# An interleaved decoder trunk on eight cores: first loads in one queue by need, a late query filler, and schedule priorities found by search

## The chip, the cores and the metric

The kernel runs on all eight cores of one Trainium2 chip. Each core computes its own piece of the sequence. The time is the device time of the slowest core, in microseconds (us). The program has a second, slower state, in which one die, or both, is granted a lower TensorE clock in the records (0.84 in one such execution, 3153 us).

## The reference, cut to what matters

```python
DEPTH = 4; D_MODEL = 1024; SEQ = 8192; BATCH = 2; N_META = 16
for i in range(DEPTH):                       # mixers: attention, convolution, pooling, attention
    a = rms_norm(h, norm_mix[i])
    m = (sliding_window_attention | short_conv_mixer | pooling_mixer)(a, ...)
    h = h + m
    h = h + swiglu(rms_norm(h, norm_ffn[i]), gate[i], up[i], down[i])   # the FFN
h = rms_norm(h, norm_final)
```

A norm needs the squares of all 1024 channels (ScalarE), their sum (a product with ones on TensorE), a reciprocal root (ScalarE) and eight multiplications (VectorE, tag `apply`) before the products behind it can start.

## The kernel before: the parts that matter

The activations stay on the core. The columns are split into three groups, and four layers by three groups make twelve steps. While one step's FFN runs, the next step's mixer can run beside it. The mixer of the first layer is attention: it needs three projections (products of the normed x with weights) called K, V and query, and K and V also of the halo, 192 columns of x from before the core's own piece. The kernel records every operation with a duration and a priority `v`, and when it is built, a list scheduler orders each engine's instructions. For each engine it looks for the earliest possible start, and among the operations that could start then it takes the lowest `v`:

```python
for t, o in cands:
    if t <= mt + 1e-6 and (bo is None or (o.pv, o.id) < (bo.pv, bo.id)):
        bo = o
...
if FILL and e == "pe" and t - free["pe"] > FILL_MIN:      # FILL_MIN = 1500 ns
    self.fill(free["pe"], t)        # 128x128 products of constants, result unread
```

The filler is meant to keep the clock of TensorE up: in the trace of the kernel before, the granted clock was at half from 19.7 to 33.3 us, around a bare wait of 9.3 us. Priorities follow a fixed rule: a mixer of step `s` is spread over `s` to `s + 0.8`, its FFN's norm has `s + 0.9`, the FFN is spread over `s + 1` to `s + 2`, and the final norm of a group has `s + 1.9`:

```python
def end_segment(g, v0, span):
    tot = sum(o.dur for o in g.seg if o.eng == "pe") or 1.0
    c = 0.0
    for o in g.seg:
        o.v = v0 + span * c / tot
        if o.eng == "pe":
            c += o.dur
```

Weights come through a ring buffer, issued by GpSimd in order of need. The activations and constants are issued by SyncE, and later x blocks wait for chosen operations:

```python
xa = load_x(0, 4, v=-9.0)                        # first x block, four pieces, SyncE
load(gam[:], gam_d, ["gam"], v=-8.95)            # eight more small constants like it
...
def LATER():                                     # next group's x, gated by the last statistics op
    w = [o for o in g.ops if o.tag == LTAG]
    w = [w[LIDX]]
    for t in (2, 3):
        load_x(t, 1, after=w, v=-8.0)
    load_tables(0, after=w, v=-7.9)
...
for t in (2, 3):                                 # query filler: the next group's query products
    norm_to(aM, "aM", 0, TILES[t][0], TILES[t][1], GROUPS[1][0], v=QB_NV)       # QB_NV = None
...
q_tile(u, 0, 1, c, TILES[t][0], TILES[t][1], v=QB_V)                            # QB_V = None
```

The softmax here doesn't subtract the row's maximum and nothing guards it: scores larger than these inputs give would overflow.

Of the kernel before, what the change touches and what calls it, by code (L numbers as in the profile page):

```python
# [11 lines left out]
KC = 8  # L12
# [15 lines left out]
SPAN = (0.8, 0.8, 0.8)  # L28
NV = (0.9, 0.9, 0.9)
ITERS = 1  # L30


def JIT(s, sp, nv):
    return sp, nv


VORDER = True
# [3 lines left out]
VOFF = 0.0  # L41
QB_AT = 0
LTAG = "stat"
LIDX = -1
UA = {0: (1,),1:(3,),2:(4,)}
QB_NV = None
QB_V = None
# [4 lines left out]
RING = 16400  # L52

# [91 lines left out]
class Op:  # L145
    __slots__ = ("eng", "dur", "ins", "raw", "war", "v", "vts", "nleft", "succ", "start", "fin", "vis", "idx", "ready",
                 "id", "dma", "clock", "pv", "extra", "nbytes", "unit", "tag")


class Unit:  # L150
    __slots__ = ("src", "n", "users", "left", "off", "order", "dop", "first", "v", "arr", "grp", "num")


class G:
    def __init__(self):
        self.ops = []
        self.keys = {}
        self.units = []
        self.v = 0.0
        self.seg = None  # L160
        self.unit_after = {}
# [7 lines left out]
    def op(self, eng, dur, ins, R=(), W=(), after=(), dma=None, unit=None, v=None, tag="", hold=(), war_after=(), gate=()):  # L169
# [7 lines left out]
        o.id = len(self.ops)  # L177
        raw = {}
# [65 lines left out]
        o.v = self.v if v is None else v  # L244
# [19 lines left out]
    def weights(self, src, n, grp=None):  # L264
        u = Unit()
        u.grp = grp if grp is not None else len(self.units)
        u.num = len(self.units)
        u.src = src
        u.n = n
        u.users = []  # L270
        u.first = None
        self.units.append(u)
        return u
# [6 lines left out]
def end_segment(g, v0, span):  # L280
    tot = sum(o.dur for o in g.seg if o.eng == "pe") or 1.0
    c = 0.0
    for o in g.seg:
        o.v = v0 + span * c / tot
        if o.eng == "pe":
            c += o.dur
    g.seg = None

# [36 lines left out]
class Scheduler:  # L325
# [30 lines left out]
    def run(self, ring_mode=True):  # L356
# [18 lines left out]
        for o in g.ops:  # L375
            for vt in o.vts:
                vt.left = len(vt.users)
                vt.slot = None
            if o.nleft == 0:
                ready[o.eng].append(o)  # L380
# [13 lines left out]
        def place():  # L394
# [3 lines left out]
            u = uorder[nu]  # L398
            off = ptr
# [15 lines left out]
            for q in g.unit_after.get(nu, ()):  # L415
                if q.start is None:
                    return None
                t = max(t, q.vis)
            return u, off, deps, max(t, pool_t)

        def issue(nxt):
            nonlocal nu, ptr, dma_t, pool_t
            u, off, deps, t = nxt
            dset = set(id(x) for x in deps)
            live[:] = [x for x in live if id(x[2]) not in dset]
            st = max(dma_t, t + 200.0)
            pool_t = max(t + 530.0, st - 12000.0)
# [4 lines left out]
            self.uload.append((u, deps, t, g.unit_after.get(nu, ())))  # L432
            live.append((off, u.n, u))
            ptr = off + u.n
            nu += 1

        gates = set(q.id for l in g.unit_after.values() for q in l)
        self.nfill = 0
        pool_t = 0.0
# [3 lines left out]
        while nsched < total:  # L443
# [39 lines left out]
            if nxt is not None and (best is None or nxt[3] <= best[0]):  # L483
                issue(nxt)
# [34 lines left out]
            if o.unit is not None:  # L519
                u = o.unit  # L520
                if u.first is None:
                    u.first = nsched
                    for q in u.users:
                        if q.start is None and q.pv > o.pv:
                            q.pv = o.pv
                u.left -= 1
            for vt in o.vts:
                vt.left -= 1
                if vt.left == 0:
                    self.pools[vt.pool].release(vt)  # L530
            for s, war in o.succ:
                r = o.vis + self.lat(o, s, war)
                if r > s.ready:
                    s.ready = r
                s.nleft -= 1
                if s.nleft == 0:
                    ready[s.eng].append(s)
            if ring_mode and nxt is None and ((o.unit is not None and o.unit.left == 0) or o.id in gates):
                nxt = place()
# [3 lines left out]
def late_starts(g, s, T):  # L543

    L = {}
    nxt = {}
    for e in ENGS:
        q = s.seq[e]
        for a, b in zip(q[:-1], q[1:]):
            nxt[a.id] = b  # L550
    xs = {}
    for o in g.ops:
        for q in o.extra:
            xs.setdefault(q.id, []).append(o)
    over = {}
    for i, (u, deps, st, after) in enumerate(s.uload):
        for u2 in deps:
            over.setdefault(id(u2), []).append(i)
    ldma = {}
    items = [(o.start, 1, o.id, o) for o in g.ops] + [(st, 0, i, u) for i, (u, d, st, af) in enumerate(s.uload)]  # L560
    items.sort(key=lambda x: (-x[0], x[1], -x[2]))
    lastd = T
    for st, kind, i, o in items:
        if kind == 0:
            f = min([L[q.id] for q in o.users] or [T]) - DMA_LAT
            f = min(f, lastd)
            lastd = f - o.n * 512 / DMA_RATE
            ldma[i] = lastd
            continue
        f = T  # L570
        for q, war in o.succ:
            f = min(f, L[q.id] - s.lat(o, q, war) - (DMA_LAT if o.dma is not None else 0.0))
        for q in xs.get(o.id, ()):
            f = min(f, L[q.id] - s.lat(o, q, True))
        n = nxt.get(o.id)
        if n is not None and o.dma is None:
            f = min(f, L[n.id])
        if o.unit is not None:
            for j in over.get(id(o.unit), ()):
                if j in ldma:  # L580
                    f = min(f, ldma[j] - 200.0)
        L[o.id] = f - (o.fin - o.start if o.dma is None else o.dur)
    return L


def unit_order(g):
    m = {}
    for u in g.units:
        m[u.grp] = min(m.get(u.grp, 1 << 60), u.first)
    return sorted(g.units, key=lambda u: (m[u.grp], u.num))  # L590


def try_run(g, make_pools, order):
    s = Scheduler(g, make_pools(), order)
    t = s.run(ring_mode=order is not None)
    return s, t


def schedule(g, make_pools, iters=None):
    iters = iters or ITERS  # L600
    s, t = try_run(g, make_pools, None)
    order = unit_order(g)
    best = None
    v0 = [o.v for o in g.ops]
    if VORDER:
        m = {}
        for u in g.units:
            m[u.grp] = min([m.get(u.grp, 1e18)] + [o.v + VOFF * (o.tag in ("gate", "up", "down")) for o in u.users])
        order = sorted(g.units, key=lambda u: (m[u.grp], u.num))
    hist = []  # L610
    for it in range(iters):
        try:
            s, t = try_run(g, make_pools, order)
        except RuntimeError as ex_:
            hist.append("dead")
            g.dead = str(ex_)
            if best is None:
                raise
            break
        hist.append(round(t / 1e3, 1))  # L620
        if best is None or t < best[0]:
            best = (t, [o.v for o in g.ops], list(order))
        order2 = unit_order(g)
        if it >= 2:
            L = late_starts(g, s, t)
            for o in g.ops:
                o.v = L[o.id]
        order = order2
    g.hist = hist
    for o, v in zip(g.ops, best[1]):  # L630
        o.v = v
    s, t = try_run(g, make_pools, best[2])
    return s, t


def emit(nc, g, s, pools, ring, n_dma_sems=24):
# [16 lines left out]
    for i, (u, deps, st, after) in enumerate(s.uload):  # L653
# [4 lines left out]
        uops.append((st, 0, i, u, (deps, after)))  # L658
# [38 lines left out]
    def deps_of(o, dp):  # L697
        if isinstance(o, Unit):
# [3 lines left out]
            r.extend(dp[1])  # L702
# [110 lines left out]
def build():  # L813
# [6 lines left out]
    x_d = din("x", [128, KC * NCOL])  # L820
    xh_d = din("xh", [128, KC * 192])
    gam_d = din("gammas", [128, 9 * KC])
    flag_d = din("flags", [128, 2])
    onesf_d = din("onesf", [128, 128])
# [6 lines left out]
    ab_d = din("attn_b", [2, 128, 18])  # L831
    abv_d = din("attn_bv", [2, 128, 512])
    eb_d = din("attn_eb", [2, 128, 4 * 1024])
# [4 lines left out]
    cw_d = din("conv_w", [128, 3 * KC])  # L838
    pw_d = din("pool_w", [128, 4 * 2 * 256])
    psc_d = din("pool_scale", [128, KC])  # L840
    pic_d = din("pool_invc", [128, KC * NMETA])
# [41 lines left out]
    gam = sb("gam", [128, 9 * KC])  # L883
    flags = sb("flags", [128, 2])
# [5 lines left out]
    onesf32 = sb("onesf32", [128, 128])  # L890
    attb = sb("attb", [128, 2, 18])
    attbv = sb("attbv", [128, 512])
    cw = sb("cw", [128, 3 * KC])
    psc = sb("psc", [128, KC])
    pic = sb("pic", [128, KC * NMETA])
# [38 lines left out]
    def load(dst, src, W, after=(), v=0.0):  # L934
        nload[0] += 1
        nb = 1
        for x_ in dst.shape:
            nb *= x_
        return g.op("sp", nb * 4 / DMA_RATE, lambda e: e.dma_start(out=dst, in_=src), W=W, dma="ld%d" % nload[0], after=after,
                    v=v, tag="load")  # L940
# [3 lines left out]
    def load_x(ti, halves, after=(), v=0.0):  # L944
        c0, c1 = TILES[ti]
        w = c1 - c0
        base = KC * c0
        nk = KC // halves
        r = []
        for q in range(halves):  # L950
            k0 = q * nk
            r.append(load(hraw[:, base + k0 * w:base + (k0 + nk) * w], x_d[:, base + k0 * w:base + (k0 + nk) * w],
                          [("h", k, ti) for k in range(k0, k0 + nk)], after=after, v=v))
        return r

    xa = load_x(0, 4, v=-9.0)
    load(gam[:], gam_d, ["gam"], v=-8.95)
    load(attb[:, 0, :], ab_d[0], [("attb", 0)], v=-8.94)
# [925 lines left out]
```

## Time and profile before

| | before |
|---|---|
| time, median of three executions, one of them slow | 2779.7 us |
| span of the profiled core | 2778.4 us |
| busy: TensorE, VectorE, ScalarE | 2710.0, 1591.2, 1336.7 us |
| of TensorE's busy time, filler | 64.5 us |
| idle plus filler of TensorE: 0 to 33.5 us, to 250 us, middle, tail | 28.7, 34.3, 55.9, 14.0 us |

The first thing to see is that TensorE is busy 98% of the time, so there is no wait to remove that would bring much. The second is that 64.5 us of this is filler. A better order can win filler and idle time. The lines of these views stand in the prediction below.

### The profile page before, as it was taken

To read this page: it belongs to the slowest core of one execution; us is meant where nothing else is said; L and a number is where in the kernel's file an instruction comes from. 1 tells how busy PE (TensorE), PEld (TensorE's weight loads), DVE (VectorE), ACT (ScalarE), POOL (GpSimd) and SP (SyncE) were. 2 spreads that over 40 slices of the span, in tenths; PEclk is the share of its full clock that TensorE was granted. 3 is DMA by queue.
4 is the path that set the end of the run, shared out by engine and by line. 5 is a ranking of instruction groups with operands and counts; after the bars stand their busy time and mean duration, and the time that the engine had idled before them with its cause. 6 is when DMAs were issued, how large, how long until landed. Compare 5 with 4: busy or idle time off the path is not lost.

```text
span 2778.4 us, 53437 instructions; the slowest of 8 cores (2762.9 to 2778.4 us)
## 1 busy us (share of the span) xinstructions
PE 2710.0 (98%) x19034; PEld 1720.0 (62%) x19034; DVE 1591.2 (57%) x3267; ACT 1336.7 (48%) x2632; POOL 496.4 (18%) x940
## 2 busy tenths in 40 slices
PE   7899999999999999999999999999999999999998
PEld 6556665556665666666566666656666767556654
DVE  3577445755447446544895686545565566464534
ACT  5675545635244333524444454544564664564533
POOL 1011221111211121112111221112112122111110
PEclk8999999999999999999999999999999999999999
DMA  9375875666676677567566787667677769547763
GB/s 219 47 123 95 125 116 79 97 95 100 100 121 97 97 118 114 92 105 114 76 90 105 107 117 142 103 97 110 97 107 112 121 105 165 92 67 118 127 99 78
DMA packets 145554, 297.80 MB, mean 107 GB/s; under 512 B 16912, under 2 KB 23440, under 8 KB 144528
## 3 DMA queue, kind: packets, MB, share of 16 engines
q0 software_dynamic: 134064, 270.07, 64.0%
q1 hardware_dynamic: 11232, 24.33, 2.7%
q8 instruction: 158, 2.59, 0.4%
q14 instruction: 100, 0.82, 0.1%
HBM read 555.95 MB, written 8.39 MB: 203 GB/s over the span
## 4 chain that ended last, share of the span: by engine, by line
PE 91%; DVE 3%; ACT 2%; issue 2%; DMA 2%; SPq 0%; DVEq 0%; ACTq 0%
PE ps L1069 85%; PE ps L1266 1%; PE ps L1231 1%; DMA sb_h<-x 1%; PE ps L1166 1%; PE ps L1272 1%; DVE sb_P L1241 1%; PE ps L1556 1%; DVE sb_h L1623 1%; ACT ps L1236 1%; DMA sb_ms<-attn_ebm 0%; DVE sb_t L1604 0%; PE ps L980 0%; ACT sb_t L1602 0%; ACT sb_t L1598 0%
## 5 line engine op out<-in xcount | busy, mean ns | idle before, releaser
L1069 PE MATMUL ps<-sb_aF,sb_ring 128*128 128x384 bf16 (+3 forms) x8576 | 1365.8, 317 | 19.2 <-DVE sb_t L1604 11.3
L1069 PEld LDWEIGHTS ps<-sb_aF,sb_ring 128*128 128x128 bf16 x8576 | 830.8, 98 | 508.3 <-issue 48.3
L1069 PE MATMUL ps<-sb_g,sb_ring 128*128 128x384 bf16 (+4 forms) x4400 | 688.0, 316 | 5.0 <-DVE sb_g L1608 3.1
L1069 PEld LDWEIGHTS ps<-sb_g,sb_ring 128*128 128x128 bf16 x4400 | 426.7, 98 | 250.6 <-issue 15.7
L1598 ACT ACTIVATE sb_t<-ps 128x384 f32<-128x384 f32 (+3 forms) x528 | 243.8, 463 | 634.6 <-PE ps L1069 633.2
L1604 DVE TENSOR_TENSOR sb_t<-sb_t,ps 128x384 f32<-128x384 f32 (+3 forms) x528 | 277.9, 528 | 462.7 <-ACT sb_t L1602 452.2
L789 POOL DMA_DIRECT2D sb_ring<-ffn_gu x528 | 279.7, 534 | 1037.2 <-PE ps L1069 870.1
L1608 DVE TENSOR_TENSOR sb_g<-sb_t,ps 128x384 bf16<-128x384 f32 (+3 forms) x528 | 277.0, 527 | 222.8 <-PE ps L1069 218.2
L1080 DVE TENSOR_TENSOR sb_h<-ps,sb_h 128x384 f32<-128x384 f32 (+3 forms) x432 | 226.3, 530 | 186.4 <-PE ps L1069 182.5
L1069 PE MATMUL ps<-sb_aM,sb_ring 128*128 128x384 bf16 (+2 forms) x1952 | 326.6, 318 | 4.5 <-ACT sb_ms L1433 2.5
L1600 ACT ACTIVATE sb_t<-sb_t,sb_ones 128x384 f32<-128x384 f32 (+3 forms) x528 | 312.1, 592 | 31.9 <-ACT sb_t L1598 0.4
L1602 ACT ACTIVATE sb_t<-sb_t 128x384 f32<-128x384 f32 (+3 forms) x528 | 263.8, 500 | 29.2 <-ACT sb_t L1600 0.8
L990 ACT ACTIVATE sb_sq<-sb_h 128x768 bf16<-128x768 f32 (+3 forms) x216 | 167.8, 801 | 221.3 <-DVE sb_h L1080 150.4
L1069 PEld LDWEIGHTS ps<-sb_aM,sb_ring 128*128 128x128 bf16 x1952 | 188.6, 98 | 118.4 <-issue 11.0
L789 POOL DMA_DIRECT2D sb_ring<-ffn_dn x192 | 101.6, 534 | 546.2 <-PE ps L1069 516.7
L1241 DVE TENSOR_TENSOR sb_P<-ps,sb_ms 128x1024 bf16<-128x1024 f32 x124 | 150.9, 1222 | 59.2 <-ACT ps L1236 58.2
L1069 PE MATMUL ps<-sb_qo,sb_ring 128*128 128x384 bf16 (+2 forms) x1024 | 169.2, 317 | 0.4 <-DVE sb_P L1241 0.4
L1236 ACT ACTIVATE ps<-ps 128x1024 f32<-128x1024 f32 (+1 forms) x134 | 133.7, 1002 | 62.9 <-PE ps L1231 62.0
L1069 PEld LDWEIGHTS ps<-sb_qo,sb_ring 128*128 128x128 bf16 x1024 | 99.6, 98 | 57.2 <-issue 1.9
L1035 DVE SCALAR_TENSOR_TENSOR sb_aF<-sb_h,sb_gam,sb_rs 128x384 bf16<-128x384 f32 (+3 forms) x192 | 101.7, 586 | 6.3 <-ACT sb_rs L1013 5.9
L1003 DVE TENSOR_TENSOR sb_sq<-sb_sq 128x768 bf16<-128x768 bf16 (+3 forms) x156 | 82.7, 530 | 35.1 <-ACT sb_sq L990 33.2
L1464 ACT ACTIVATE sb_ms<-sb_ms,sb_cw 128x384 f32<-128x384 f32 (+2 forms) x48 | 28.8, 601 | 131.5 <-DVE sb_ms L1459 128.6
(122 smaller groups left out, 1538.4 us busy)
## 6 DMA issues: line engine op xcount, KB each, us to landing
sb_ring<-ffn_gu POOLq DMA_DIRECT2D x528, 256.0 KB, 6.2
sb_ring<-ffn_dn POOLq DMA_DIRECT2D x192, 352.0 KB, 5.6
sb_ring<-conv_in POOLq DMA_DIRECT2D x72, 256.0 KB, 5.1
sb_ring<-attn_o POOLq DMA_DIRECT2D x48, 256.0 KB, 6.1
sb_ring<-attn_q POOLq DMA_DIRECT2D x40, 256.0 KB, 7.2
sb_ring<-attn_k POOLq DMA_DIRECT2D x12, 512.0 KB, 5.6
sb_ring<-attn_v POOLq DMA_DIRECT2D x12, 512.0 KB, 5.9
sb_ring<-conv_out POOLq DMA_DIRECT2D x24, 256.0 KB, 9.1
```

Of the source, the lines that this page charges most:

```text
L789: e.dma_start(out=ring[:, o.off:o.off + o.n], in_=o.src).then_inc(sem(o.dop[0]), 16)
L990: lambda e, sv=sv, c=c: e.activation(out=ap(sv)[:, 0:2 * n].rearrange("p (a b) -> p a b", a=2), in_=src(2 * c, 2 * c + 2), func=AF.Square),
L1035: lambda e, k=k: e.scalar_tensor_tensor(out=dst[:, k, c0 - goff:c1 - goff], in0=h1(k, c0, c1), scalar=gam[:, gi * KC + k:gi * KC + k + 1], ...
L1069: i = e.matmul(bank(pv)[:, 0:n], lhsT=wap(u, woff + k * wst, M), rhs=rhs(k), start=(k == 0), stop=(k == nk - 1))
L1080: f = lambda e: e.tensor_tensor(out=h1(m, c0, c1), in0=bank(pv)[:, 0:n], in1=h1(m, c0, c1), op=ALU.add)
L1236: g.op("act", act_ns(4 * W), lambda e: e.activation(out=sp3(), in_=sp3(), func=AF.Exp, scale=0.125), R=[S], W=[S], tag="exp")
L1241: g.op("dve", dve_ns(4 * W), lambda e: e.tensor_tensor(out=pp(), in0=sp3(), in1=ebt, op=ALU.mult), R=[S, ("eb", p)], W=[Pv], tag="ebmul", ...
L1598: g.op("act", act_ns(n), lambda e, pg=pg, tv=tv, n=n: e.activation(out=ap(tv)[:, 0:n], in_=bank(pg)[:, 0:n], func=AF.Exp, scale=-1.0), R=[ ...
L1600: g.op("act", act_ns(n, True, True), lambda e, tv=tv, n=n: e.activation(out=ap(tv)[:, 0:n], in_=ap(tv)[:, 0:n], func=AF.Ln, bias=ones1[:], ...
L1602: g.op("act", act_ns(n, True), lambda e, tv=tv, n=n: e.activation(out=ap(tv)[:, 0:n], in_=ap(tv)[:, 0:n], func=AF.Exp, scale=-1.0), R=[tv] ...
L1604: g.op("dve", dve_ns(n), lambda e, pg=pg, tv=tv, n=n: e.tensor_tensor(out=ap(tv)[:, 0:n], in0=ap(tv)[:, 0:n], in1=bank(pg)[:, 0:n], op=ALU ...
L1608: g.op("dve", dve_ns(n), lambda e, pu=pu, tv=tv, n=n, fj=fj, a=a, b=b: e.tensor_tensor(out=gg[:, fj, a - goff:b - goff], in0=ap(tv)[:, 0:n ...
```

## The change

Three things are changed. First loads: x blocks and constants leave SyncE's queue and stand at named places in GpSimd's queue between the weights, small constants come in two pieces, GpSimd's memsets go to VectorE, and the K and V weights of the first group are loaded once. Query filler: the next group's query products, which need nothing of this group, get a late priority. Priorities: the rule becomes a table with its own numbers for each of the twelve steps and an offset for each kind of operation, searched offline against the scheduler's own estimate of the end.

```diff
-SPAN = (0.8, 0.8, 0.8)
-NV = (0.9, 0.9, 0.9)
+PLACE = {
+    "mix": [(-0.001, 0.825), (-0.179, 0.945), (-0.068, 0.637), ...],   # 12 pairs (cut)
+    "norm": [(0.867, 0), (0.942, 0), (0.954, 0), ...],
+    "ffn": [(0.96, 1.063), (1.032, 1.024), (0.998, 1), ...],
+}
+BOOST = {"den": 0.12, "hadd": -0.04, "vt": 0.184, "z": -0.098, ...}    # 21 kinds (cut)
-QB_NV = None
-QB_V = None
+QB_NV = 0.44
+QB_V = 0.52
+FINV = 3.5
+ATS = {"A0": ("K",) * 4, "cst": "K", "eb": ("Q0", "O1"), "X": "Q2", "A1": ("Q5",) * 2,
+       "B0": ("Q6",), "B1": ("Q6",), "C0": (1.2, 1.3), "C1": (1.4, 1.5), "cst2": 1.6}
@@ (priorities) @@
+            a, b = PLACE[kind][step]
+            o.v = step + a + b * rel
+        o.v += BOOST.get(o.tag, 0.0)
@@ (loads) @@
-        return g.op("sp", nb * 4 / DMA_RATE, ..., dma="ld%d" % nload[0], after=after, v=v, tag="load")
+        o = g.op("sp" if at is None else "pool", nb * 4 / DMA_RATE, ..., tag="load")
+        if at is not None:
+            o.slotted = True
+            g.slots.append((o, at))
@@ (query weights of the first group) @@
+                    u.boost = QB_V is None
@@ (memsets) @@
-    g.op("pool", 3000, lambda e: e.memset(KX[:], 0.0), ...)
+    g.op("dve", 1000, lambda e: e.memset(KX[:], 0.0), ...)
@@ (final norm) @@
-            final(gi, s_ + 1.9)
+            final(gi, s_ + (FINV if gi < 2 else 1.9))
```

(Cut: the packing of the constants, key names, an exponential of the tables split into smaller pieces, the scheduler's handling of GpSimd's queue, which goes with the loads, and the layout of x in HBM, where each piece that is loaded now lies together.)

## The prediction

> **What bounds the kernel now.** I read the page first, then the span cut into four stretches for all instructions and for the filler alone, then TensorE's waits, the chain that ended last, and the timeline around the fillers.
>
> ```profile
> PE 2710.0 (98%) x19034; PEld 1720.0 (62%) x19034; DVE 1591.2 (57%) x3267; ACT 1336.7 (48%) x2632; POOL 496.4 (18%) x940
> DMA  9375875666676677567566787667677769547763
> ```
>
> TensorE is the bound, and the 98% is too kind: line 980 is a filler, a 128x128 product of constants whose result nobody reads, placed by the kernel's own list scheduler wherever it expects TensorE to idle for over 1.5 us. Filler and idle together are what a better order can win. All engines by stretch:
>
> ```profile
> 0.00:33.50 33.50, 19.29 (x158) 15.80 (x159) 7.79 (x21) 10.53 (x17) 10.85 (x21) 0.69 0.93 226
> 33.50:250.00 216.50, 200.91 (x1783) 131.13 (x1781) 141.73 (x258) 150.35 (x299) 25.94 (x49) 0.99 0.62 112
> 250.00:2764.00 2514.00, 2487.92 (x17074) 1571.55 (x17071) 1430.97 (x2969) 1172.90 (x2312) 459.62 (x870) 1.00 0.67 105
> 2764.00:2778.40 14.40, 1.94 (x26) 1.49 (x25) 10.69 (x21) 2.95 (x5) 0.00 (x0) 0.74 0.61 219
> ```
>
> and the filler alone (first number after the length is TensorE):
>
> ```profile
> 0.00:33.50 33.50, 14.53 (x138) 14.49 (x139) 0.69 0.93 226
> 33.50:250.00 216.50, 18.74 (x312) 17.38 (x309) 0.99 0.62 112
> 250.00:2764.00 2514.00, 29.77 (x501) 28.89 (x501) 1.00 0.67 105
> ```
>
> Idle plus filler: start 14.2 + 14.5 = 28.7 us; to 250 us 15.6 + 18.7 = 34.3 us; the long middle 26.1 + 29.8 = 55.9 us; the tail 12.5 + 1.5 = 14 us. The chain says what the large ones wait for, and the timeline shows two fillers:
>
> ```profile
> 6.72 19.77 DMA sb_h<-x
> 166.34 11.02 DMA sb_h<-x
> 1415.94 6.92 DMA sb_ring<-ffn_gu
> ```
> ```profile
> 1408.81 5.80 PE L980 MATMUL ps<-sb_onesb 128*128 128x128 bf16 x101
> 2588.29 6.86 PE L980 MATMUL ps<-sb_onesb 128*128 128x128 bf16 x120
> ```
>
> At the start TensorE waits for activations x that share the DMA with weights and tables not yet needed; at 166 us for x blocks that a gate issues late. At 1409 us VectorE, 45 to 50 us busy of 50 from 1350 to 1450, makes the pooling mixer too late. At 2588 us VectorE does the final norm of a finished group (line 1623) while the FFN's products queue behind it. The other waits of the middle are short:
>
> ```profile
> PE ps L1069 <- DVE sb_t L1604: 10.5, 13, 2.2
> PE ps L1069 <- DVE sb_g L1608: 4.2, 5, 1.3
> ```
>
> **The floor.** Intervals from the start of one matmul to the next are, in the middle of the trace, 163 ns for 384 columns, 109 for 256, 176 for 416: columns / 2.4 + 2.8 ns; matmuls that use half of the array run two at a time. Summed over the 18064 useful matmuls of the built program that is 2589.6 us, the same before and after (the instruction orders have the same number and shapes). Each change between whole and half array costs another 0.10 us (median over some 400 such changes).
>
> **What the Trainium skill says.** "TensorE: Matmul & The Clock Gate", section "Wait — 56ns, not 53.3ns?", gives N / 2.4 GHz + about 2.5 ns warm and N / 1.2 cold; the trace agrees: fillers start 56 ns apart, 107 ns in the first 6 us, and 163 ns for 384 columns. "TensorEngine Tiling (Array Packing)", section "Key Properties", says that a change of tiling mode drains TensorE; the 0.10 us per change agrees. "DMA: Bandwidth & Descriptors", section "Issuing engines are not separate DMA queues", says that transfers started by several engines interleave on the same 16 DMA engines. The trace agrees: with both queues busy, the two 512 KB pieces of x issued by SyncE take 21.2 us from issue to landing. So one queue in order of need can bring the first needed bytes sooner without moving more of them per second.
>
> **The change part by part.**
>
> *First loads.* All x blocks and constants leave SyncE's queue and stand in GpSimd's queue between the weights; nine small constants become one 375 KB piece and one 91 KB piece; GpSimd's memsets go to VectorE; K and V weights of the first group are loaded once instead of twice, 2.1 MB less (counted as read, float32). Before, I count 20.3 MB read by 68 us, or 307 GB/s, with the DMA share at 0.93 to 0.95: the start is bandwidth-bound, so order matters. With a first landing near 3.5 us and 307 GB/s, the changed order lands: first x block (1.70 MB) 9 us, constants 10, K 14, V 17, bias tables 22, first query weights 24 to 26, halo 29, three more query weights 34, second x block 37, next group's x 44 and 49, last query weights 52. Before, the first K projection starts at 33.6 us, behind halo and second block; in the changed order it stands ahead of both. First block in at 9 to 10, statistics and reciprocal root 2 us (11.4 to 13.7 before), eight applies of 0.6 us: K could start at 17. But 107 fillers stand before it, and the clock was half from 9.5 to 16.3 us before; at 107 then 56 ns they last to about 19. So the first 33.5 us lose not 28.7 but 17 to 18 before K, then perhaps 6 in waits for query weights, second block and halo. After that the order has fillers of 65, 25, 23 and 23, at 56 ns 7.6 us, and I allow 6 us of short waits and x delays that the order can't show: 31 of start loss against 63.0. Gain 32 us. The 11.02 us load at 166 us disappears from the chain, because those blocks now stand among the first FFN's weights.
>
> *Query filler at low priority.* The next group's query projections (384 columns) fill holes in the first group's attention. Before, they alternate with the group's own queries from 57 us on and are used up; now they come after its first attention units. No work is added; its worth is in the 31 above.
>
> *Priorities.* Of the 501 fillers of the middle the changed order has none: no row of line 980's successor stands between about 105 us of useful work and the last norm. Their 29.8 us, the 8 us that stood between a filler's end and the next useful matmul (differences of starts: 38 us in all), and three half-clock windows of 3.4 us, worth 1.7 us each where TensorE works through them, should go: 43 us. Of the roughly 20 us of other waits, I guess that a search that counts them too takes 6, and that new ones below the filler's threshold of 1.5 us cost 5. Gain 44 us.
>
> *Cost.* The finer interleaving raises the whole/half array changes from 402 to 436: 34 x 0.10 = 3.4 us more.
>
> *Tail.* The last rows of all engines are the same: eight squares, two statistics, 16 applies. Nothing.
>
> Sum: 2778.4 - 32 - 44 + 3.4 = 2705.8 us of span; the measured 2779.7 is 1.3 above its span, so 2707 us, 2.6% less.
>
> **Rivals.** (1) GpSimd's single queue becomes the wait: each issue takes 0.53 us there (mean 534 ns), one that waits for ring space holds all behind it, and x blocks now stand behind weights. For it: GpSimd's weight issues already wait for TensorE for some 2 ms in sum. Against: the first block stands first, and later x blocks are placed far ahead of need. The start would win 10 us instead of 32: 2729. (2) The searched order fits its model and not the chip: priorities tuned to fractions of a microsecond, with switches of the array left out of the model. For it: the model put the second x block earlier than it came (a bare 9.3 us wait at 17.9 us, with no filler). Against: away from the first loads nearly every filler of before ends 0.5 us before the next useful matmul, so the model knows the chip's waits. Fillers would turn into unfilled waits, half of the middle's gain: 2729. (3) The search also empties the short waits, and the start is as good as the bytes allow (25 us lost): 2589.6 + 43.6 + 25 + 14 + 8 = 2680. (4) DMA in the middle becomes the bound: its share there is 0.67 and bytes do not rise, so hardly.
>
> **Range and chances.** The line at 2% is 2724. Either rival 1 or 2 alone lands just above it, with neither I land below. Predicted 2707, range 2682 to 2734; faster by over 2% 0.77, within 2% 0.225, slower by over 2% 0.005, since useful work and tail do not change and no part can cost over 50 us.
>
> **What would show it.** Right: filler busy near 18 to 22 us instead of 64.5; idle plus filler of the middle near 15 to 20 us instead of 55.9; the first K projection at 17 to 21 us; the first 250 us losing 25 to 40 us; no x in the chain at 166 us; no idle behind the final norm; TensorE's useful busy time up by 3 us or less. Wrong: a K projection after 25 us, a long DMA item in the chain between 20 and 70 us (rival 1), or waits on VectorE of 1 to 3 us that sum to over 40 us in the middle (rival 2).

## The result and the profile after

| | before, same rounds | after |
|---|---|---|
| fast executions | 2778.1 to 2779.7 us | 2713.1 to 2715.9 us |
| median of four, one of them slow | 2779.6 us | 2715.4 us |
| ratio, 95% interval | | 0.9768 [0.9746, 0.9790] |
| filler, all of TensorE | 64.5 us | 23.5 us |

A ratio is the mean time of one kernel's fast executions over the mean of the other's in the same rounds, so it is not quite the ratio of the medians. The change is faster by 2.3% (the case given 0.77), within the predicted range and 8 us above the predicted 2707.

The first page of the profile of the changed kernel, busy time by engine and the DMA's share in 40 slices:

```profile
PE 2668.3 (98%) x18380; PEld 1675.6 (62%) x18380; DVE 1592.5 (59%) x3272; ACT 1337.2 (49%) x2646; POOL 501.1 (18%) x952
DMA  8396775757787687667766877866667767757683
```

The 98% is unchanged, and alone it would suggest that nothing happened. The count of matmuls tells more: it is 654 lower, and this is the filler, 316 instead of 970. The same span by stretch (length, busy time of PE, PEld, DVE, ACT, POOL, which are TensorE's products, its weight loads, VectorE, ScalarE and GpSimd, then granted clock, DMA share, GB/s), first for all instructions, then for the filler alone (PE, PEld, clock, DMA share, GB/s):

```profile
0.00:33.50 33.50, 26.74 (x241) 20.76 (x241) 14.41 (x25) 15.66 (x29) 15.18 (x32) 0.90 0.93 215
33.50:250.00 216.50, 205.65 (x1756) 127.61 (x1755) 154.02 (x280) 158.40 (x319) 29.01 (x55) 1.00 0.64 111
250.00:2699.60 2449.60, 2434.00 (x16361) 1525.75 (x16359) 1413.43 (x2947) 1160.23 (x2294) 456.91 (x866) 1.00 0.71 107
2699.60:2714.00 14.40, 1.93 (x25) 1.49 (x25) 10.65 (x21) 2.95 (x5) 0.00 (x0) 0.77 0.62 219
```
```profile
0.00:33.50 33.50, 13.75 (x157) 13.48 (x157) 0.90 0.93 215
33.50:250.00 216.50, 8.29 (x136) 7.61 (x136) 1.00 0.64 111
250.00:2699.60 2449.60, 0.00 (x0) 0.00 (x0) 1.00 0.71 107
```

Length minus busy time is idle time, and with the filler it gives: first 33.5 us 6.8 + 13.75 = 20.5 (before 28.7); to 250 us 10.9 + 8.3 = 19.1 (34.3); middle 15.6 + 0 = 15.6 (55.9); tail 12.5 + 1.45 = 13.9 (14.0). Summed, the start gained 23.4 us, the middle 40.3, the tail nothing. TensorE's busy time without filler went from 2645.6 to 2644.8, another 0.7 us. That is all of the 64.4 us by which the profiled spans differ.

In the chain that ended last (start, length, what), these are the DMA items of the changed kernel up to 300 us and one late one:

```profile
3.32 8.04 DMA sb_h<-x
181.56 11.60 DMA sb_h<-x
218.51 10.34 DMA sb_h<-x
...
2275.39 13.00 DMA sb_ring<-attn_q
```

The 19.77 us item of x at the start is gone; what is left is the 8.04 us in which the first x block arrives. The later x blocks are still in the chain, twice. An item of the chain is not an idle TensorE, though: from 175 to 240 us its waits are one of 1.9 us and one of 0.2, and from 215 to 230 us it is busy without a gap. The late query weights hold it for 3.2 us of the 13. That is not all that they cost: the clock was at half from 2287.4 to 2294.2 us, and over the wait and this stretch TensorE lost 6.4 us by the measure of the next section, the largest single loss in the changed kernel's middle.

TensorE's waits of the middle (what waited, for what: us in total, times, longest):

```profile
PE ps L1018 <- DVE sb_t L1562: 6.6, 9, 1.4
PE ps L1018 <- DVE sb_g L1566: 3.2, 4, 0.9
PE ps L1018 <- DMA sb_ring<-attn_q: 3.2, 1, 3.2
```

The two waits on VectorE were 10.5 and 4.2 us before. The one long wait for a DMA (2.8 us before, for an FFN's weights) is now for query weights; no other wait of the middle sums to over 0.7 us.

The timeline of TensorE around the first K projection, before and then after (start, length, instructions):

```profile
28.61 5.13 PE L980 MATMUL ps<-sb_onesb 128*128 128x128 bf16 x48
33.57 1.48 PE L1069 MATMUL ps<-sb_g,sb_ring 128*128 128x192 bf16 x16
```
```profile
13.14 8.26 PE L929 MATMUL ps<-sb_onesb 128*128 128x128 bf16 x107
21.23 1.52 PE L1018 MATMUL ps<-sb_g,sb_ring 128*128 128x400 bf16 x8
```

The K projection stands 12.3 us earlier. Where the kernel before had a filler of 120 products at 2588 us, after a final norm, the changed kernel works on without a gap:

```profile
2526.08 19.18 PE L1018 MATMUL ps<-sb_aF,sb_ring 128*128 128x384 bf16 x117
```

### The profile page after: what moved, and what is told of

Same layout as the page of the kernel before. It is cut to its first block, busy times and chain, and to the rows that moved or that the text cites. A ratio compares the mean times of both kernels' runs of the same rounds, so it can differ in the third digit from the quotient of the medians.

```text
span 2714.0 us, 52156 instructions; the slowest of 8 cores (2704.4 to 2714.0 us)
## 1 busy us (share of the span) xinstructions
PE 2668.3 (98%) x18380; PEld 1675.6 (62%) x18380; DVE 1592.5 (59%) x3272; ACT 1337.2 (49%) x2646; POOL 501.1 (18%) x952
## 4 chain that ended last, share of the span: by engine, by line
PE 93%; DMA 2%; DVE 2%; ACT 1%; issue 1%; POOL 0%; DVEq 0%; ACTq 0%; SPq 0%; POOLq 0%
PE ps L1018 87%; PE ps L1216 1%; PE ps L1181 1%; DMA sb_h<-x 1%; PE ps L1116 1%; PE ps L1222 1%; DMA sb_ms<-attn_ebm 0%; DMA sb_ring<-attn_q 0%; PE ps L1514 0%; DVE sb_P L1191 0%; PE ps L929 0%; ACT sb_sq L939 0%; DVE sb_h L1581 0%; ACT ps L1186 0%; DMA sb_ring<-pool_w 0%
## 5 line engine op out<-in xcount | busy, mean ns | idle before, releaser
L1018 PE MATMUL ps<-sb_aF,sb_ring 128*128 128x384 bf16 (+3 forms) x8576 | 1359.8, 316 | 10.5 <-DVE sb_t L1562 8.5
L1018 PEld LDWEIGHTS ps<-sb_aF,sb_ring 128*128 128x128 bf16 x8576 | 827.6, 98 | 497.2 <-issue 40.4
L1018 PEld LDWEIGHTS ps<-sb_g,sb_ring 128*128 128x128 bf16 x4400 | 426.3, 98 | 249.6 <-issue 15.7
L1560 ACT ACTIVATE sb_t<-sb_t 128x384 f32<-128x384 f32 (+3 forms) x528 | 263.4, 500 | 28.7 <-ACT sb_t L1558 0.4
L1186 ACT ACTIVATE ps<-ps 128x1024 f32<-128x1024 f32 x134 | 133.8, 1001 | 33.1 <-PE ps L1181 32.1
L984 DVE SCALAR_TENSOR_TENSOR sb_aF<-sb_h,sb_cst,sb_rs 128x384 bf16<-128x384 f32 (+3 forms) x192 | 101.8, 588 | 14.3 <-ACT sb_rs L962 13.3
L1031 DVE SCALAR_TENSOR_TENSOR sb_h<-ps,sb_cst,sb_h 128x384 f32<-128x384 f32 (+3 forms) x144 | 82.8, 587 | 31.2 <-PE ps L1018 29.8
```

Of the source, the lines that this page charges most:

```text
L984: lambda e, k=k: e.scalar_tensor_tensor(out=dst[:, k, c0 - goff:c1 - goff], in0=h1(k, c0, c1), scalar=gam[:, gi * KC + k:gi * KC + k + 1], ...
L1018: i = e.matmul(bank(pv)[:, 0:n], lhsT=wap(u, woff + k * wst, M), rhs=rhs(k), start=(k == 0), stop=(k == nk - 1))
L1186: g.op("act", act_ns(4 * W), lambda e: e.activation(out=sp3(), in_=sp3(), func=AF.Exp, scale=0.125), R=[S], W=[S], tag="exp")
L1560: g.op("act", act_ns(n, True), lambda e, tv=tv, n=n: e.activation(out=ap(tv)[:, 0:n], in_=ap(tv)[:, 0:n], func=AF.Exp, scale=-1.0), R=[tv] ...
```

## The experiments

All twelve kernels gave correct results, and all profiled executions were fast. To place a loss, I use one measure for all of them: the **lost time**, clock minus useful work, where a useful matmul counts as columns / 2.4 + 2.8 ns (pairs on half of the array as one). It is read at 200 us of useful work, which is about 255 to 284 us on the clock, and at the last useful matmul; the tail of 14 us behind that is not in it. Filler, idle time, half clock and changes of the array's shape are all in it. It comes from one execution each, and the split carries some noise: e7 and e8 have the change's order but for a filler and the first loads, and read 1.5 and 3.3 us more by 200 us and 2.2 and 2.8 us less after it.

| kernel | fast executions, us | lost by 200 us of work | lost after that |
|---|---|---|---|
| before | 2778.1 to 2779.7 | 83.8 | 90.7 |
| the change | 2713.1 to 2715.9 | 59.8 | 50.3 |
| e1 loads only | 2768.8 (2791.6) | 72.1 | 91.3 |
| e2 priorities only | 2742.3 to 2746.9 | 81.9 | 59.0 |
| e3 final norm early | 2728.3 to 2732.6 | 60.0 | 61.5 |
| e4 query not late | 2735.9, 2738.3 | 75.5 | 54.0 |
| e5 loads and late query | 2769.4, 2770.7 | 74.8 | 89.4 |
| e6 no offsets | 2744.1 to 2746.1 | 78.0 | 60.9 |
| e7 half the second filler | 2716.1 | 61.3 | 48.1 |
| e8 first block by SyncE | 2716.7 | 63.1 | 47.5 |
| e9 priorities moved by 0.001 | 2754.7 to 2756.6 | 63.9 | 86.9 |
| e10 search with array changes | 2710.4 to 2712.0 | 65.9 | 39.3 |
| e11 search with late start | 2704.8 to 2706.4 | 54.8 | 45.3 |
| e12 the same, another seed | 2705.4 to 2706.9 | 61.2 | 39.9 |

The kernel before took 2777 to 2785 us in its fast executions in the rounds beside them.

### e1: the loads alone

```diff
+PLACE = {"mix": [(0.0, 0.8)] * 12, "norm": [(0.9, 0)] * 12, "ffn": [(1.0, 1.0)] * 12}
+BOOST = {}
-QB_NV = 0.44 ; QB_V = 0.52 ; FINV = 3.5
+QB_NV = None ; QB_V = None ; FINV = 1.9
```

> Only the loads of the change (one GpSimd queue in order of need, constants in pieces, K and V of the first group once); all priorities as before, query filler at its old priority, final norm as before. The built order has 835 fillers (before 970, changed 316), 443 of them in the middle. Theory A (the two parts add up: start about 24 us, middle about 40 us, as the two traces split it): 2754 to 2764 us, loss at 200 us of useful work near 62 us, middle idle plus filler still near 50 us. Theory B (the order of the loads is hidden or eaten by the slower GpSimd path, and the whole gain is the priorities'): 2772 to 2782 us.

One clean execution of 2768.8 us, 11 less than before (the second one that counts as fast, 2791.6, had two cores at 0.982 and 0.984 of the clock, and it makes the ratio, 1.0002 [0.9932, 1.0072], useless). The profiled span of 2767.1 us agrees. The lost time is 11.7 us less at the start and the same afterwards: the loads alone are worth 11 to 12 us, about half of the start's gain and between the two theories. What of it is the order, and what the 2.1 MB that are no longer loaded (an estimate: 7 us at the 307 GB/s that the prediction counted), no run separates.

### e2: the priorities alone

The kernel before with the table, the offsets and the later final norm, and with its own loads and its own query filler.

```diff
-def end_segment(g, v0, span):
+def end_segment(g, kind, step):
...
-        o.v = v0 + span * c / tot
+        a, b = PLACE[kind][step]
+        o.v = step + a + b * c / tot
...
+    for o in g.ops:
+        o.v += BOOST.get(o.tag, 0.0)
...
-            final(gi, s_ + 1.9)
+            final(gi, s_ + (FINV if gi < 2 else 1.9))
```

> Kernel before with the loads as they were and only the searched priorities (steps, operation boosts, late final norm). 501 fillers in the built order, 54 of them in the middle. Theory A: the middle gain alone, 2735 to 2743 us, start loss as before (near 84 us at 200 us of useful work). Theory B: nearly the whole gain, 2715 to 2725 us. If the sum of the gains of this run and of loads_only falls short of 64 us by more than 8, the parts need each other.

Ratio 0.9874 [0.9857, 0.9891], 35 us. The start gains 1.9 us, the rest 31.7. So the two parts alone sum to 46 us, and all three parts together give 64.

### e3: the final norm at its old priority

```diff
-FINV = 3.5
+FINV = 1.9
```

> Changed kernel with the final norm of the first two groups back at its old priority; nothing else. The order gets 43 + 56 + 102 + 21 fillers in the last layer (222 at 56 ns, 12.4 us). Theory A (VectorE's final-norm applies delay the FFN products, TensorE waits): 2726 to 2734 us. Theory C (VectorE has room, the wait is only moved): within 3 us of the changed kernel's 2715.

Ratio 0.9825 [0.9801, 0.9848], about 15 us slower than the change (12 us in the profiled spans). The start is the same to 0.2 us. At 2400 us of useful work it has lost 108.7 us against 107.7, at 2500 us 119.7 against 107.7, so nearly all of it lies around the last final norm before the tail. In the timeline of TensorE there, the filler of before is back:

```profile
2536.40 5.86 PE L929 MATMUL ps<-sb_onesb 128*128 128x128 bf16 x102
2542.68 2.60 PE L1018 MATMUL ps<-sb_aF,sb_ring 128*128 128x384 bf16 x15 [0.42 <-DVE sb_g L1566]
```

VectorE does the final norm of a finished group while the FFN's VectorE work waits behind it, as the prediction read it from the kernel before. One constant is worth about a fifth of the whole gain.

### e4: the query filler at its old priority

```diff
-QB_NV = 0.44 ; QB_V = 0.52
+QB_NV = None ; QB_V = None
```

> Changed kernel with the next group's query projections back at the old, high priority; nothing else. The order has 481 fillers instead of 316: 112 instead of 23 at 93 us of useful work, 31 again late in the pooling layer. Theory A (the query work is used up too soon and is missing in the holes of the attention that follows): 165 fillers at 56 ns, so 2722 to 2728 us. Theory D (the start is bound by the bytes, so the order of its work is worth nothing): 2713 to 2718 us.

Ratio 0.9847 [0.9823, 0.9871], about 22 us slower than the change, more than either theory had. Of it 15.7 us lie in the start. TensorE's filler to 250 us is 27.8 us instead of 22.0, and eight waits of attention for VectorE's product of probabilities and bias sum to 5.7 us (in the change four, 2.0 us): the holes in the first group's attention are there again, and the work that could fill them is used up.

### e5: loads and late query, flat priorities

```diff
 (as e1, but)
+QB_NV = 0.44 ; QB_V = 0.52
```

> The loads of the change and the low priority of the query filler, all other priorities as before. The runs so far: loads alone about 11 us, priorities alone 35, both without the low query priority 43, all three 64: the low query priority is worth 20 us beside the others. Theory E (it needs only the loads: the query work fills the first group's attention): 2750 to 2758 us, loss at 100 us of useful work near 50 us. Theory F (it needs the searched priorities too, above all the operation boosts: with the flat ones the built order has 898 fillers against 835 of loads alone, and again 112 at 93 us of useful work): 2766 to 2778 us, loss at 100 us above 60.

2769.4 and 2770.7 us, ratio 0.9961 [0.9941, 0.9981]: no better than the loads alone. The late query by itself is worth nothing. It is worth 20 us beside the table and the offsets.

### e6: no offsets by kind

```diff
-BOOST = {"den": 0.12, "hadd": -0.04, "vt": 0.184, ...}
+BOOST = {}
```

> Changed kernel without the boosts by kind of operation; the step priorities stay. The order has 548 fillers (44, 70 and 112 in the first 93 us of useful work, 56 + 21 late). Theory F (the boosts keep the query filler for the later holes): start loss 12 to 18 us worse than the changed kernel's 60 at 200 us of useful work, total 2730 to 2738 us. Theory E: below 2724 us.

Ratio 0.9874 [0.9857, 0.9890], 30 us slower than the change and slower than expected. The start loses 18.2 us more and the rest 10.6. Nearly two thirds of what the offsets bring lie in the first 200 us of useful work. That they decide there between work of this group and of the next is a reading, not shown by itself.

### e7: half of the second filler

```diff
-            n = int((b - a - FILL_END) / pe_ns(128) * (0.5 if self.clock.half else 1.0))
+            n = int((b - a - FILL_END) / pe_ns(128) * (0.5 if self.clock.half or self.nfill == 1 else 1.0))
```

> Changed kernel with 53 instead of 107 fillers between the first statistics and the first K projection. The applies that K waits for ended at 19.44 us and K started at 21.23, after the fillers, so K should start 1.6 us earlier, at 19.5 to 19.8. Theory G (the query weights, the halo and the second block gate what follows): nothing left of it at 40 us of useful work, total 2713 to 2717. Theory H (each us of delay of K goes through to the end): total 1.6 us less.

The trace of the changed kernel shows the applies done at 19.4 us and K at 21.2, with fillers between: the scheduler put in 107, which take 6.0 us at 56 ns each, but the clock was at half from 10.7 to 17.5 us and they took 8.1. With 53 of them, K starts when its data is there (timeline of TensorE, filler and K):

```profile
13.13 4.05 PE L929 MATMUL ps<-sb_onesb 128*128 128x128 bf16 x53
19.68 1.51 PE L1018 MATMUL ps<-sb_g,sb_ring 128*128 128x400 bf16 x8 [2.50 <-DVE sb_g L984]
```

K is 1.55 us earlier, and at 40 us of useful work the lost time is 37.9 us against 38.1: the gain is gone before the second x block is worked through. One execution, 2716.1 us. What the start waits for after K are bytes, and an earlier K meets them earlier.

### e8: the first block by SyncE

```diff
-ATS = {"A0": ("K",) * 4, "cst": "K", ...}
+ATS = {"A0": (None,) * 4, "cst": None, ...}
...
-    g.op("dve", 1000, lambda e: e.memset(KX[:], 0.0), ...)      # and VU, VW
+    g.op("pool", 1700, lambda e: e.memset(KX[:], 0.0), ...)
```

(and GpSimd's first weight issue held back to 4.5 us; in the trace it came at 5.09)

> Changed kernel with the first x block and the constants back in SyncE's queue and the three large memsets back on GpSimd, so that its K weights are issued after 4.5 us; all later loads as in the change. Before, the last quarter of the block was used at 10.35 us; changed at 11.45. Theory I (the GpSimd path costs the first block its 1 us): first square at 6.4, last at 10.4 us, K at 20 to 20.3 us instead of 21.2, the total within 2 us of the changed kernel's, as what follows is gated by later bytes. Theory J (the block is slow because weights queue behind it at once): no earlier than 11 us.

In the change, then in this run, ScalarE's square of the last quarter of the first x block:

```profile
11.45 0.90 ACT L939 ACTIVATE sb_sq<-sb_h 128x832 bf16<-128x832 f32 x1 [1.19 <-DMA sb_h<-x]
```
```profile
11.30 0.90 ACT L939 ACTIVATE sb_sq<-sb_h 128x832 bf16<-128x832 f32 x1 [1.09 <-DMA sb_h<-x]
```

The first quarter is worked on 0.9 us earlier (6.36 instead of 7.23 us), the last one 0.15 us. One execution, 2716.7 us. So the issuing engine isn't what makes the first block late. By its number this is theory J, but not by its mechanism: from 3.0 to 11.4 us GpSimd's queue moved only 0.12 of 2.05 MB here. What else differs from the kernel before, where the last quarter was used at 10.35 us (one piece of constants instead of several, the layout of x, weights that waited for pieces of x), was not tried.

### e9: every priority moved a little

All 60 numbers of the table that the search had set and the 21 offsets, moved by a normal deviate of standard deviation 0.001, which is a thousandth of a step, some 0.2 us of work.

```diff
-    "mix": [(-0.001, 0.825), (-0.179, 0.945), (-0.068, 0.637), ...
+    "mix": [(-0.000905, 0.82625), (-0.179931, 0.945992), (-0.068259, 0.636738), ...
```

> Changed kernel with every searched priority and boost moved at random by about 0.001 of a step (normal, one fixed seed); nothing else. Its built order has 863 fillers instead of 316, all 547 more of them in the middle: 92 and 128 at 772 us of useful work, 83 and 142 at 1263, 25, 56 and 21 later; the start has the same. Theory K (the gain of the priorities is that of one point found by search among neighbours that are far worse, not of a rule that the numbers express): 547 fillers at 56 ns are 31 us, so 2742 to 2756 us, start loss as in the changed kernel. Theory L (the chip's own waits decide and a thousandth of a step is nothing): 2712 to 2720 us.

Ratio 0.9903 [0.9879, 0.9927], 41 us slower than the change. The start keeps all but 4 us of its gain; the middle loses 36.6. The filler alone in the middle stretch, which was 0.00 (x0):

```profile
250.00:2740.00 2490.00, 31.68 (x547) 31.12 (x547) 1.00 0.70 105
```

This is as much filler as before the change, and by its number it is theory K. But the holes are few. In the timeline of TensorE, 445 of the 547 stand in two places, each before the products of an FFN whose norm comes too late:

```profile
844.73 5.30 PE L922 MATMUL ps<-sb_onesb 128*128 128x128 bf16 x92
850.38 7.31 PE L922 MATMUL ps<-sb_onesb 128*128 128x128 bf16 x128
1348.47 4.80 PE L922 MATMUL ps<-sb_onesb 128*128 128x128 bf16 x83
1353.60 8.09 PE L922 MATMUL ps<-sb_onesb 128*128 128x128 bf16 x142
```

The lost time grows there by 13 and by 20 us, most of the 36.6; elsewhere it follows the change's. And e2 and e6, which stand much further from the searched point, keep 31.7 and 29.8 us of the 40.4 that the change wins after 200 us. So the table is worth something away from its point too, but having no hole at all is a property of that one order, and a thousandth of a step can open two large ones. It is one draw, so how bad neighbours are on average is open. It also limits what e4 and e6 say: taking a piece away also moves the order off its point, and part of their losses can be of this kind. (The loss of e3 lies at the norm that it moves.)

### e10: the search again, with the array change in the scheduler

The scheduler's durations leave out what a change between whole and half array costs. I put in 0.10 us for each (and for changes between two shapes of half array) and searched the same 81 numbers again, from those of the change.

```diff
+SWITCH = 100.0
+HALF = {"score": 1, "scorem": 1, "av": 2, "avm": 3, "vmeta": 4}
...
-                o.fin = clock.run(t, o.dur) if e == "pe" else t + o.dur
+                if e == "pe":
+                    mode = HALF.get(o.tag, 0)
+                    o.fin = clock.run(t, o.dur + (SWITCH if mode != self.mode else 0.0))
+                    self.mode = mode
```

> Changed kernel with its priorities searched again, by random steps from those of the change, in the same scheduler with one thing added to it: 0.10 us for each change between whole and half array, as the trace before shows it. Loads, operations and fillers as in the change. With that cost in it the scheduler's own end time is 2710.6 us for the change and 2680.8 us for this one; the order has 392 array changes instead of 436 (4.4 us) and the rest is fewer waits. Theory M (what the search could not see was the changes of the array; the schedule's end follows on the chip): 2682 to 2692 us. Theory N (the search fits its model and not the chip): 2705 to 2725 us.

2710.4 to 2712.0 us, ratio 0.9745 [0.9728, 0.9762]. The middle is 11 us better than the change's, and the start gives 6 of it back. This is theory N's range. The scheduler's first loads land earlier than those of the chip, so an order tuned to it may miss at the start; the next two runs try this.

### e11 and e12: the search with what the traces showed

```diff
 (as e10, and)
-DMA_RATE = 330.0
+DMA_RATE = 325.0                  # 310.0 in e12
-        dma_t = 0.0
+        dma_t = 3000.0
```

(and the halved second filler of e7)

> The changed kernel with its priorities searched again, this time against a model of the scheduler that has three things the traces of the earlier runs showed: 0.10 us for each change of array shape, first transfers landing 3 us later, and the rate of 325 bytes per ns that the landings showed. 388 changes of array shape, 200 filler matmuls. Theory P (what was missing in run e10_search_with_switch was the start, and an order tuned to the landings of the chip keeps both gains): 2685 to 2700 us, at least 14 us under the changed kernel's 2715, with the loss up to the 200th us of useful work at or below the changed kernel's 60 us (e10 had 66) and about 40 us or less after it. Theory Q (the scheduler's durations are too rough for an order to be tuned closer than this; every search ends near 2710 on the chip): 2705 to 2720 us.

> The same search from another seed and with a slower rate of 310 bytes per ns, so a different order (402 changes of array shape, 212 filler matmuls). It tells whether the result of e11_search_late_start is that of one lucky point. Theory P: again 2685 to 2702 us. Theory Q: 2705 to 2720 us, and then the two differ by chance only.

Fast executions of 2704.8 to 2706.4 us (three; three were slow) and 2705.4 to 2706.9 (four; four slow), ratios 0.9737 [0.9720, 0.9755] and 0.9740 [0.9727, 0.9753]. Both are 8 to 9 us below the change, though they weren't timed in the same rounds as the change. The 2685 to 2700 of theory P did not come: by the ranges it is theory Q, at its lower edge. The start of e11 is what P said (54.8 us lost, K at 19.3 us), its middle is not (45.3 instead of 40 or less); in e12 it is the other way round (61.2 and 39.9). So the late landings in the model did not make the start better both times, and that they were what e10 lacked is not shown. Two different orders from the same kind of search end within 1 us of each other. Stretches of e11's filler alone, start and to 250 us:

```profile
0.00:33.50 33.50, 11.29 (x128) 11.06 (x128) 0.95 0.94 214
33.50:250.00 216.50, 1.74 (x28) 1.56 (x28) 1.00 0.65 115
```

Of 8.3 us of filler between 33.5 and 250 us 1.7 are left. Whether a search could be brought closer to the chip than this stays open.

## Why the prediction was right or wrong

**The bound: right.** TensorE's work without filler did not change (2645.6 and 2644.8 us), and all but 0.7 us of the gain came out of filler and idle time.

**The middle: right, for its mechanism and its size.** Predicted were 44 us less 3.4 for array changes, 40.6; measured are 40.3 us of idle and filler and 0.7 us of busy time. The filler of the middle is 0, and its idle plus filler is 15.6 us, inside the 15 to 20 that were named. The final norm's part (e3) is confirmed. The 3.4 us for array changes can be checked in the two traces: I count 404 changes of the array's shape before and 438 after (about a fifth of them between two shapes of half array, which the prediction's words leave out), with a median of 0.09 to 0.10 us each beyond the usual interval, 38.1 and 42.0 us in sum. The three half-clock stretches of 3.4 us of the middle are gone, but one of 6.8 us came at 2287.4 us. e10, whose order has 392 changes, is 11 us better in the middle, for that reason and others.

**The start: the mechanism right, the gain too large by 8.6 us.** This is the step that failed: "31 of start loss against 63.0. Gain 32 us". Measured are 39.6 and 23.4. Most of it is a slip of addition. The terms that the text names are 17 to 18 us before K, 6 in waits for query weights, second block and halo, 7.6 in fillers and 6 in short waits. They sum to 37, not to 31; it looks as if one of the two sixes was dropped. With the right sum the gain is 26 and the time 2713, 2 us from the measured 2715.4. Term by term: before K, 13.75 us of filler and 5.4 us of idle time are 19.2 (predicted 17 to 18); after it, 39.6 - 19.2 = 20.4 us (19.6). Of the signs that the prediction named, two were missed narrowly: filler 23.5 us (18 to 22) and K at 21.2 us (17 to 21).

**First x block at 9 us: wrong.** Its last quarter is used at 11.45. The assumed 307 GB/s from 3.5 us on, all of it for x, did not hold. The DMA view of 3.0 to 11.4 us, the whole and the issue of the constants (KB each, us to landing):

```profile
DMA packets 402, 2.11 MB, mean 251 GB/s; under 512 B 72, under 2 KB 72, under 8 KB 402
...
sb_cst<-cst POOLq DMA_DIRECT2D x1, 366.0 KB, 9.1
```

The engines moved 2.11 MB at 251 GB/s, of which the first block is 1.70 MB; the other 0.4 MB belong to transfers issued behind it. Being first in the queue does not mean to land alone. Since e8 changes the queue and its last quarter lands only 0.15 us earlier, the queue of GpSimd isn't the cause. That the block lands at 11 us because of the first microseconds' rate is how I read it; no run isolates it. K at 21.2 instead of "about 19" follows from this (its applies end at 19.4 us instead of 17) and from 1.8 us of filler too many, which e7 shows to cost nothing in the end. The later landings came in the predicted order, at first 1 to 3 us late and from 44 us on within 1 us: V 20.1 us (17), halo 30.4 (29), second x block 39.7 (37), the next group's x 44.7 and 49.8 (44 and 49), the last query weights 52.6 (52).

**"The 11.02 us load at 166 us disappears from the chain": wrong as a statement.** Two such loads stand in the chain, 11.60 us at 181.56 and 10.34 at 218.51. They cost TensorE 1.9 us, where the stretch of before had a filler of 3.1 us before it and a clock of 0.91 behind it. The prediction took an item of the chain for lost time; the waits of TensorE are what counts.

**The query filler: its size was not given, and it is worth more than the part it was given to.** The prediction folded it into the start's 31. Without it 22 us are lost (e4), and without the table and the offsets it brings nothing (e5). The parts of this change don't add: 11 and 35 us alone, 64 together.

**Rival 1 (GpSimd's queue as the wait): fell by its signs.** K came at 21.2, not after 25, no long DMA item stands between 20 and 70 us in the chain, and e8 changes the queue of the first loads for nothing. **Rival 2 (the order fits its model, not the chip): fell for this order, but for a reason that the prediction had not weighed.** The order that was found does hold on the chip: no filler, short waits. But e9 shows that a very small move of the numbers can open two large holes, and e10 to e12 show that a better model brings 3 to 9 us and not what the better model promises. **Rival 3 (short waits emptied too): half of it.** The middle's idle plus filler is 15.6 us, and the tail's 14 us are added to the 110 us that the table of the experiments shows as lost.

## What to carry to other kernels

When the bounding engine is busy 98% of the time, subtract filler, find idle time by stretch, and ask of every part of a change which stretch it can empty; then add the terms up twice. A schedule searched against a model is one point: test it by moving its numbers a little, and search again whenever a duration, a buffer or a load changes. An item in the chain that ended last is a candidate, and only the waits of the bounding engine say what it costs.

## What the Trainium skill lacked or had wrong

- "TensorEngine Tiling (Array Packing)", section "Key Properties", says that a mode change drains TensorE and gives no size. Here it is 0.09 to 0.10 us each (median over some 400 changes), 38 us in the kernel before, nearly as much as the middle's whole gain.
- "TensorE: Matmul & The Clock Gate", section "Seeing it yourself", says to budget 1.95 GHz (13/16) for sustained dense matmuls on all cores, held while the load lasts. In the fast executions of the changed kernel all eight cores were granted 0.996 to 0.998 of the full clock with TensorE 98% busy; only some executions had a die lower (0.838 to 0.839 in that of 3153 us). The lowest, one of 3302 us of the kernel before, had a die at 0.811 to 0.819, which is about 13/16.
- "DMA: Bandwidth & Descriptors", section "Latency and other measured facts", has about 1 us to the first byte for transfers issued by GpSimd and 0.6 us for SyncE's. The difference agrees: from the start of the issue to the end of ScalarE's wait for the first quarter of x are 4.34 us (1.59 to 5.93) by GpSimd and 3.99 (1.07 to 5.06) by SyncE. What it lacks is that GpSimd starts to issue 0.5 us later (1.59 instead of 1.07 us), 0.9 us after the end of its small memsets; why, no run here shows.
- No page that I used says how much of later transfers of one queue moves before an earlier one has landed: 0.4 of 2.11 MB here, while the first block of 1.70 MB arrived.
